# A feed-forward layer in a float32 decoder trunk: fourteen pairs of column blocks computed by halves instead of ten, with another product order and another order of the weight pieces

## The chip, the cores and the metric

The kernel runs on one core of a Trainium2 chip. A core has TensorE (matrix products, PE in the profile; its weight loads are PEld), VectorE (DVE), ScalarE (ACT), GpSimd (POOL) and SyncE (SP, which here only starts transfers). Each engine runs its own instructions in program order and waits on semaphores for the others. The metric is device time in microseconds (us) for one execution; lower is better. PSUM, where matrix products accumulate, is used by banks that hold 128 x 512 float32 each.

## The reference

A decoder trunk of two layers on 512 tokens of 1024 numbers: a recurrent block in layer 0, an RWKV-7 time mixing in layer 1, and behind each a gated feed-forward network with a causal convolution. The change is in the feed-forward network alone:

```python
def _conv_ffn(x, norm, w_up, conv_w, conv_b, w_down):
    h = _rmsnorm(x, norm)
    u = jnp.einsum('btd,df->btf', h, w_up)
    gate = _causal_dwconv(u[..., :D_FF], conv_w, conv_b)
    hid = jax.nn.gelu(gate, approximate=True) * u[..., D_FF:]
    return jnp.einsum('btf,fd->btd', hid, w_down)
```

`D_FF` is 3072, so `w_up` is 1024 x 6144 (3072 gate columns, then 3072 up columns) and `w_down` 3072 x 1024. The convolution runs along the tokens, with three taps.

## The kernel before, in words

**Precision.** Every matrix product is in float32 by three products of rounded operands (`mm3`, L54): a weight w is split into a rounded high part and the rest, `wh` and `wl` (or `hi` and `lo`), and so is x. The split is a cast on ScalarE (L94, or L747 for `hi`) and a subtraction on VectorE (L97, or L748 for `lo`).

**Pairs.** A feed-forward layer is cut into 12 pairs, n = 0 to 11. A pair is 256 gate columns and the 256 up columns that belong to them. A pair is computed in one of two ways.

- `Whole`: four steps G0, U0, G1, U1, where G is gate, U is up and 0 and 1 are the halves of the 1024 rows; 24 matmuls of 128 x 512 in each step.
- `Halves`: the tokens, the 1024 rows and the two kinds of columns (gate and up) are all cut in two, and seven products, numbered 1 to 7, of sums and differences of the halves replace eight (a Strassen-like scheme). Each is 24 matmuls of 128 x 256. `HALVES = (3, 5, 7, 9, 11)` names these pairs, in both layers, so that there are ten.

**Banks in a `Halves` pair.** Products 1, 6, 7 and 4 go one after another into bank A (`accA`), each added to what is there; behind 1, 6 and 7 ScalarE copies the bank to a tile `s[1]`, `s[6]`, `s[7]` (L769). Product 5 and then 3 go into bank F (`accF`), product 2 into bank D (`accD`). VectorE adds D to s[1] (L771), F behind product 5 to s[7] (L775) and F behind product 3 to s[6] (L778); the gate half goes to `gpad` (L776, L782). Then come the convolution (`cv`, L692 and L694), the gelu (`ge`, L695), the product with the up half (L787) and the split of the hidden tile (`hid`, L788 and L789).

**Weights.** `plan` lists all weight pieces in the order in which they are fetched. `weights_load` starts a 512 KB transfer on SyncE's queue (L166) into a `raw` tile and, for two of the five pieces of a `Halves` pair, a second transfer on GpSimd's queue that adds another piece into the tile (L168). The operand of product 6 is the sum of the raw tiles of products 1 and 5 (VectorE, L741), formed in the tile of product 1; GpSimd then adds one more piece into the same tile, for product 3 (L752). So a raw tile serves products 1, 6 and 3 one after another. The tiles of raw, hi, lo, wh and wl all come from one pool of 21 rooms, and a new tile waits until the last reader of its room is done.

**Order.** `products` walks through the list of (pair, product) and prepares the weights of two products ahead. For n = 3, 5, 7, 9, 11 the loop at the end of the layer runs the products of pairs n - 1 (`Whole`) and n up to product 7, and then `down`, the products of hidden columns by `w_down`: its first piece, then products 3 and 4 of pair n (`between`), then its other pieces, at the end of the first half of which the next pair's first products are prepared (`then`). Within this a scheduler settles the order of the instructions on each engine.

## Time and profile before

| | |
|---|---|
| median of 3 runs | 1278.75 us (1278.33 to 1279.27) |
| profiled execution | 1279.1 us |
| its span | 1277.3 us |
| mean granted clock of TensorE | 0.998 |
| transferred | 141.37 MB, 111 GB/s |

The page of the profile gives the busy time of each engine, the span in 40 slices, the DMA queues, the chain of waits that ended last, and the costliest groups of instructions. A row of a timeline is start, length (us), engine, line, operation, what it writes and reads, the tile's shape, how many instructions are merged, and in brackets the time the engine stood idle before it and what it waited for. In a row of a group, the numbers behind the bar are the busy time, the mean length of one in ns, and the idle time of the engine just before. Successive matmuls overlap in the records, so the length of a product is taken as the distance from its first matmul to that of the next product. Names such as `L769` are lines of the kernel before; in the changed kernel the same statements stand a few lines lower (L747 becomes L751, L748 L752, L752 L756, L741 L743, L769 L773, L775 L779, L778 L782).

### The profile page before, as it was taken

To read this page: it belongs to the slowest core of one execution; us is meant where nothing else is said; L and a number is where in the kernel's file an instruction comes from. 1 tells how busy PE (TensorE), PEld (TensorE's weight loads), DVE (VectorE), ACT (ScalarE), POOL (GpSimd) and SP (SyncE) were. 2 spreads that over 40 slices of the span, in tenths; PEclk is the share of its full clock that TensorE was granted. 3 is DMA by queue.
4 is the path that set the end of the run, shared out by engine and by line. 5 is a ranking of instruction groups with operands and counts; after the bars stand their busy time and mean duration, and the time that the engine had idled before them with its cause. 6 is when DMAs were issued, how large, how long until landed. Compare 5 with 4: busy or idle time off the path is not lost. (4 is left out here: it accounts for less than half of the span.)

```text
span 1277.3 us, 22409 instructions
## 1 busy us (share of the span) xinstructions
PE 1256.0 (98%) x9259; PEld 1067.4 (84%) x9259; DVE 929.2 (73%) x1412; ACT 642.8 (50%) x1006; POOL 131.1 (10%) x206
## 2 busy tenths in 40 slices
PE   9999999999999999999999898999999999999998
PEld 8777888989898989877778797778889898989896
DVE  5998678767676767789999967778776666666654
ACT  6797455434343434559845356545644334343442
POOL 3000001010101010010012145310010101000000
PEclk9999999999999999999999999999999999999999
DMA  7312335445454544413222122122345454545431
GB/s 228 109 53 97 98 119 114 158 106 167 97 175 89 181 83 137 141 57 110 67 75 68 35 63 85 50 94 83 127 88 181 83 182 83 182 83 182 98 133 66
DMA packets 117829, 141.37 MB, mean 111 GB/s; under 512 B 10138, under 2 KB 91748, under 8 KB 117600
## 3 DMA queue, kind: packets, MB, share of 16 engines
q1 hardware_dynamic: 100528, 122.44, 29.9%
q0 software_dynamic: 16624, 16.47, 8.3%
q8 instruction: 72, 1.18, 0.4%
q10 hardware_dynamic: 576, 1.05, 0.2%
q14 instruction: 29, 0.24, 0.1%
HBM read 135.41 MB, written 4.52 MB: 110 GB/s over the span
## 5 line engine op out<-in xcount | busy, mean ns | idle before, releaser
L97 DVE TENSOR_TENSOR wl<-raw,wh 128x1024 fp32r<-128x1024 f32 (+1 forms) x161 | 194.4, 1213 | 123.6 <-ACT wh L94 103.8
L94 ACT CAST wh<-raw 128x1024 fp32r<-128x1024 f32 (+1 forms) x161 | 165.9, 1043 | 179.8 <-PE acc L54 40.7
L54 PE MATMUL accU<-xs,wh 128*128 128x512 f32 x448 | 138.6, 391 | 0.0
L54 PE MATMUL accG<-xs,wh 128*128 128x512 f32 x448 | 138.6, 390 | 0.0
L54 PE MATMUL acc<-hid,wh 128*128 128x512 f32 x384 | 117.9, 389 | 0.0
L748 DVE TENSOR_TENSOR lo<-raw,hi 128x1024 fp32r<-128x1024 f32 x70 | 85.5, 1222 | 39.4 <-PE accU L54 32.0
L747 ACT CAST hi<-raw 128x1024 fp32r<-128x1024 f32 x70 | 73.7, 1054 | 60.4 <-PE accU L54 25.3
L54 PEld LDWEIGHTS accU<-xs,wh 128*128 128x128 f32 x448 | 83.7, 188 | 17.1
L54 PEld LDWEIGHTS accG<-xs,wh 128*128 128x128 f32 x448 | 83.7, 188 | 17.0
L54 PE MATMUL accU<-xs,wl 128*128 128x512 f32 x224 | 87.2, 389 | 0.0
L54 PE MATMUL accG<-xs,wl 128*128 128x512 f32 x224 | 87.2, 389 | 0.0
L54 PE MATMUL accA<-xt,hi 128*128 128x256 f32 x480 | 83.5, 277 | 0.0
L54 PEld LDWEIGHTS acc<-hid,wh 128*128 128x128 f32 x384 | 71.4, 188 | 14.3
L54 PE MATMUL acc<-xs,wh 128*128 128x512 f32 x256 | 80.9, 398 | 0.0
L694 DVE SCALAR_TENSOR_TENSOR cv<-gpad,pv,cv 128x512 f32<-128x512 f32 x96 | 69.1, 747 | 13.1 <-ACT cv L692 12.7
L848 PE MATMUL acc<-wh,hid 128*128 128x512 f32 (+1 forms) x200 | 76.2, 381 | 0.0
L849 PE MATMUL acc<-wl,hid 128*128 128x512 f32 (+1 forms) x200 | 76.1, 381 | 0.0
L847 PE MATMUL acc<-wh,hid 128*128 128x512 f32 (+1 forms) x200 | 76.1, 381 | 0.0
L54 PE MATMUL acc<-hid,wl 128*128 128x512 f32 x192 | 74.3, 389 | 0.0
L168 POOL DMA_DIRECT2D raw<-in_ffn_w_up_dram x20 | 25.7, 1285 | 469.8 <-DVE x L863 166.5
L54 PEld LDWEIGHTS accA<-xt,hi 128*128 128x128 f32 x480 | 72.6, 188 | 0.0
L54 PE MATMUL accA<-xt,lo 128*128 128x256 f32 x240 | 66.3, 276 | 0.0
(411 smaller groups left out, 2938.0 us busy)
## 6 DMA issues: line engine op xcount, KB each, us to landing
raw<-in_ffn_w_up_dram SPq DMA_DIRECT2D x106, 512.0 KB, 3.9
raw<-in_ffn_w_down_dram SPq DMA_DIRECT2D x48, 512.0 KB, 4.0
raw<-in_ffn_w_up_dram POOLq DMA_DIRECT2D x30, 512.0 KB, 5.7
raw<-in_rwkv_w_rkv_dram SPq DMA_DIRECT2D x24, 512.0 KB, 3.8
raw<-in_lru_w_in_dram SPq DMA_DIRECT2D x16, 512.0 KB, 4.0
raw<-in_lru_w_out_dram SPq DMA_DIRECT2D x8, 512.0 KB, 3.8
raw<-in_rwkv_w_out_dram SPq DMA_DIRECT2D x8, 512.0 KB, 3.8
xd<-x SPq DMA_DIRECT2D x8, 256.0 KB, 2.1
```

What stands on the lines that cost most here:

```text
L54: mm = lambda *a, **kw: self.nc.tensor.matmul(ps, *a, skip_group_check=more, **kw)
L94: put = (self.nc.vector.tensor_copy if dve else self.nc.scalar.copy)(hi, src)
L97: self.nc.vector.tensor_tensor(lo, src, hi.bitcast(F32), ALU.subtract)
L168: self.nc.gpsimd.dma_start(raw, more, accum_op=ALU.add)
L694: nc.vector.scalar_tensor_tensor(cv, pair.gp[:, e, j : j + T], cw(j), cv, ALU.mult, ALU.add)
L747: nc.scalar.copy(hi, f[p])
L748: tt(lo, f[p], hi.bitcast(F32), ALU.subtract)
L847: nc.tensor.matmul(ps, hh[:, s], wh[:, k, m], start=kk == 0, stop=False)
L848: nc.tensor.matmul(ps, hl[:, s], wh[:, k, m], start=False, stop=False)
L849: nc.tensor.matmul(ps, hh[:, s], wl[:, k, m], start=False, stop=kk == blocks - 1)
```

## The change

`HALVES` becomes `(3, 5, 6, 7, 9, 10, 11)`: pairs 6 and 10 of each layer are computed by halves too. The product order of every `Halves` pair goes from 1, 5, 6, 2, 7 to 1, 2, 5, 6, 7, with 3 and 4 behind as before. In the plan the piece with an addition for product 5 comes first and the piece of product 1 second. The sum for product 6 (L743 after) gets an ordering constraint: it stands behind the last addition of F to s[6] (L782 after) of the pair that precedes. The first matmul of each half product is kept in program order (`pin`). Preparing products for the next pairs (`ahead`) is capped at product 4 of pair n until `soon` is reached in the second half of `down`; `then` only fetches the raw pieces of pair n + 1 when that is a `Halves` pair. In pairs 6 and 10 products 3 and 4 run directly behind product 7, since `down` comes only after odd pairs.

```diff
-HALVES = (3, 5, 7, 9, 11)
+HALVES = (3, 5, 6, 7, 9, 10, 11)
...
-    def mm3(self, ps, w, x, start, stop, more=False):
+    def mm3(self, ps, w, x, start, stop, more=False, pin=False):
...
-        mm(wh, xh, start=start, stop=False)
+        first = mm(wh, xh, start=start, stop=False)
+        if pin:
+            self.tc.keep_in_program_order(first)
...
-                        for first, more in (((0, 0), None), ((1, 1), (1, 0)), ((0, 1), None), ((1, 0), (0, 0)), ((1, 1), None)):
+                        for first, more in (((1, 1), (1, 0)), ((0, 0), None), ((0, 1), None), ((1, 0), (0, 0)), ((1, 1), None)):
...
-                order = ((1, 5, 6, 2, 7), (3, 4))
+                order = ((1, 2, 5, 6, 7), (3, 4))
...
-                        pair.f = dict(zip((1, 5, 2, 7), [self.loaded.pop(i + j) for j in range(4)]))
+                        pair.f = dict(zip((5, 1, 2, 7), [self.loaded.pop(i + j) for j in range(4)]))
...
-                        tt(f[1], f[5], f[1], ALU.add)
+                        add = tt(f[1], f[5], f[1], ALU.add)
+                        for ins in evicted[-1:]:
+                            tc.add_manual_dep(add.ins, ins.ins.name, NOSYNC, reason="behind the pair before")
...
-                        tt(s[6], s[6], bank["F"], ALU.add)
+                        evicted.append(tt(s[6], s[6], bank["F"], ALU.add))
...
-                while made[0] < min(j, len(seq)):
+                while made[0] < min(j, cap[0]):
...
-                    if p == "G0" and n + 1 in HALVES:
+                    if p in ("G0", 5) and n % 2 == 0 and n + 1 in HALVES:
                         self.weights_load(quads[n + 1] + 4)
...
-                    if p == 7:
+                    if p == 7 and n % 2:
                         self.weights_split(behind[n] + 2)
...
+            def fetch(n):
+                if n in HALVES:
+                    self.weights_load(quads[n] + 4)
+
+            def prepare():
+                cap[0] = len(seq)
+                ahead(at[0] + 2)
+
             for n in range(3, 12, 2):
                 products((n, 7))
+                cap[0] = seq.index((n, 4)) + 1
...
-                down(n, 2 * n - 6, 4 if n < 11 else 8, lambda: products((n, 4)), lambda: ahead(at[0] + 2))
+                down(n, 2 * n - 6, 4 if n < 11 else 8, lambda: products((n, 4)), lambda: fetch(n + 1), prepare)
```

TensorE before, in pair 5 of layer 0, at the end of product 2 (bank D) and the start of product 7 (bank A). The number behind a name tells one tile from another; what stands in brackets is the engine whose semaphore is waited for.

```order
L54 MATMUL accD<-xs_1469,hi_2581 128x256 x2
L54 MATMUL accD<-xs_1469,lo_2582 128x256
L54 MATMUL accA<-xt,hi_2612 128x256 [waits Activation_49]
L54 MATMUL accA<-xt,hi_2612 128x256
L54 MATMUL accA<-xt,lo_2613 128x256 [waits DVE_49]
```

Product 7 waits for ScalarE's copy of bank A, with product 2's 24 matmuls between the two products on that bank. TensorE after, in pair 6 of layer 0, at the end of product 6 and the start of product 7, both on bank A:

```order
L54 MATMUL accA<-xt,hi_2960 128x256 x2
L54 MATMUL accA<-xt,lo_2961 128x256
L54 MATMUL accA<-xt,hi_2994 128x256 [waits Activation_49]
L54 MATMUL accA<-xt,hi_2994 128x256
L54 MATMUL accA<-xt,lo_2995 128x256 [waits DVE_49]
```

Product 7 now follows product 6 with nothing between, and its first matmul waits for the copy. TensorE after, in the same pair, from product 7 to product 3 (bank F):

```order
L54 MATMUL accA<-xt,hi_2994 128x256 x2
L54 MATMUL accA<-xt,lo_2995 128x256
L54 MATMUL accF<-xs_1412,hi_3033 128x256 [waits DVE_49]
L54 MATMUL accF<-xs_1412,hi_3033 128x256
L54 MATMUL accF<-xs_1412,lo_3034 128x256
```

Product 3 follows product 7 at once, and waits for VectorE's addition of bank F. ScalarE after, in pair 6 of layer 0: hi_3033 and hi_3063 are the operands of its products 3 and 4, hi_3095 and hi_3125 those of products 1 and 2 of pair 7, and the three copies are those of products 1, 6 and 7.

```order
L773 COPY s<-accA 128x512 [waits PE_49]
L751 CAST hi_3033<-raw_2853 128x1024 [waits DMASW4_49,PE_49]
L751 CAST hi_3063<-raw_2992 128x1024 [waits DMAHW0_49,PE_49]
L751 CAST hi_3095<-raw_3026 128x1024 [waits DMAHW2_49,DVE_49]
L773 COPY s<-accA 128x512 [waits PE_49]
L751 CAST hi_3125<-raw_3028 128x1024 [waits DMAHW3_49]
L773 COPY s<-accA 128x512 [waits PE_49]
```

The copy behind product 6 stands behind three casts. VectorE after, at the same place, with the lo of the same operands and L779, the addition of bank F to s[7]:

```order
L752 TENSOR_TENSOR lo_3034<-raw_2853,hi_3033 128x1024 [waits DMASW4_49,PE_49,Activation_49]
L752 TENSOR_TENSOR lo_3064<-raw_2992,hi_3063 128x1024 [waits DMAHW0_49,DVE_49,Activation_49]
L752 TENSOR_TENSOR lo_3096<-raw_3026,hi_3095 128x1024 [waits DMAHW2_49,PE_49,Activation_49]
L752 TENSOR_TENSOR lo_3126<-raw_3028,hi_3125 128x1024 [waits DMAHW3_49,PE_49,Activation_49]
L779 TENSOR_TENSOR s<-s,accF 128x512 [waits Activation_49]
```

The addition on which product 3 waits stands behind the lo of pair 7's second product. Before, products 7 and 3 had the first piece of `down` between them in every `Halves` pair.

## The prediction

> **What bounds the kernel now.** I read the page first, then the table by windows for a stretch of the first FFN, then the timelines of TensorE, ScalarE and VectorE there. The page's busy times and its slices:

> ```profile
> PE 1256.0 (98%) x9259; PEld 1067.4 (84%) x9259; DVE 929.2 (73%) x1412; ACT 642.8 (50%) x1006; POOL 131.1 (10%) x206
> ...
> PE   9999999999999999999999898999999999999998
> ```

> TensorE is busy for 98% of the span, and the few slices below 9 lie in the middle, in the mixer of layer 1. The windows of the table below are two periods of layer 0's FFN, from the first matmul of pair 4 to that of pair 6, and from there to that of pair 8. A period is a `Whole` pair, a `Halves` pair and 64 matmuls by w_down, and lasts 63.1 us. The columns are busy time with instructions for PE, PEld, DVE, ACT and POOL, then the granted clock, the DMA share and GB/s.

> ```profile
> 264.10:327.20 63.10, 63.10 (x361) 55.59 (x360) 41.69 (x51) 25.05 (x30) 3.79 (x3) 1.00 0.50 134
> 327.20:390.30 63.10, 63.10 (x361) 55.59 (x360) 41.70 (x51) 25.07 (x30) 3.81 (x3) 1.00 0.50 134
> ```

> PE fills both without a hole at full clock. So in the FFN time is what the matmuls take; fewer matmul columns shorten it, and any wait of PE lengthens it, since nothing else has slack to give back. The profiled execution took 1279.1 us for a span of 1277.3; I make the sum against 1279.1 and take off 0.35 at the end, since the median of the runs is 1278.75.

> **What a converted pair gives.** TensorE's timeline gives the length of each product as the distance to the next one's first matmul:

> ```profile
> 264.12 0.62 PE L54 MATMUL accG<-xs,wh 128*128 128x512 f32 x2
> ...
> 285.88 0.40 PE L54 MATMUL accA<-xs,hi 128*128 128x256 f32 x2
> ...
> 288.75 0.40 PE L54 MATMUL accF<-xt,hi 128*128 128x256 f32 x2
> ...
> 291.49 0.39 PE L54 MATMUL accA<-xt,hi 128*128 128x256 f32 x2
> ...
> 294.21 0.39 PE L54 MATMUL accD<-xs,hi 128*128 128x256 f32 x2
> ...
> 297.07 0.40 PE L54 MATMUL accA<-xt,hi 128*128 128x256 f32 x2
> ...
> 299.81 0.63 PE L54 MATMUL acc<-hid,wh 128*128 128x512 f32 x2
> ...
> 305.26 0.40 PE L54 MATMUL accF<-xs,hi 128*128 128x256 f32 x2
> ...
> 308.13 0.40 PE L54 MATMUL accA<-xt,hi 128*128 128x256 f32 x2
> ...
> 310.87 0.63 PE L54 MATMUL acc<-hid,wh 128*128 128x512 f32 x2
> ```

> Pair 4 (`Whole`): 285.88 - 264.12 = 21.76. Pair 5 (`Halves`): products 1, 5, 6, 2, 7 take 2.87, 2.74, 2.72, 2.86, 2.74, products 3 and 4 take 2.87 and 2.74, together 19.54. A converted pair saves 2.22 us of matmul; pairs 6 and 10 in two layers make four, **-8.9 us**. That is the whole gain, and it is there only if PE still never waits.

> **What the new order adds.** Bank A is written by products 1, 6, 7 and 4, and ScalarE copies it out (L769, L773 after) behind each of 1, 6 and 7, so the next of them cannot start before the copy has ended. Before, product 5 lay between 1 and 6, product 2 between 6 and 7, and the first piece of w_down and product 3 between 7 and 4. The copies in pair 5, from ScalarE's timeline, and the two additions of bank F, from VectorE's:

> ```profile
> 294.41 0.59 ACT L769 COPY s<-accA 128x512 f32<-128x512 f32 x1 [2.91 <-PE accA L54]
> ...
> 300.01 0.59 ACT L769 COPY s<-accA 128x512 f32<-128x512 f32 x1 [0.89 <-PE accA L54]
> ```

> ```profile
> 300.63 0.69 DVE L775 TENSOR_TENSOR s<-s,accF 128x512 f32<-128x512 f32 x1 [0.25 <-ACT s L769]
> ...
> 308.33 0.69 DVE L778 TENSOR_TENSOR s<-s,accF 128x512 f32<-128x512 f32 x1 [0.79 <-PE accF L54]
> ```

> A reader of a bank starts 0.20 us after the product's end (294.41 against 294.21, 308.33 against 308.13), and the copy takes 0.59: all 0.79 us lay under product 2. In the order (1, 2, 5, 6, 7) product 7 stands right behind 6. How PE takes up work after a wait for ScalarE shows at one place outside the FFN, ScalarE's row and then TensorE's:

> ```profile
> 122.32 1.99 ACT L94 CAST wh<-raw 128x1024 fp32r<-128x1024 f32 x2
> ```

> ```profile
> 123.42 0.73 PE L54 MATMUL acc<-out,wh 128*128 128x512 f32 x2 [0.37 <-ACT wh L94]
> ```

> The first of the two casts ended about 123.37 (1.05 us each, below), PE went on 0.05 later, and its first two matmuls took 0.73 where they take 0.62 at 264.12. So a wait for a copy that starts at once costs 0.20 + 0.59 + 0.05 + 0.11 = **0.95 us**. [...]

> The places. In pairs 3, 5 and 9 four matmuls of w_down's first piece (96 of pair 4 took 21.76, so four take 0.91 us) stand between 6 and 7 and cover the copy. In pairs 6, 7, 10 and 11 nothing stands between. In pairs 6 and 10 products 3 and 4 also follow 7 directly, with no w_down piece: product 3 writes bank F, which VectorE must first add to s7, and s7 is a copy that starts at product 7's end: 0.20 + 0.59 + 0.03 + 0.69 + 0.05 + 0.11 = 1.67 us at least. So each stretch of two adjacent `Halves` pairs has three waits, at least 0.95 + 1.67 + 0.95 = 3.57 us, against 2.22 saved by that stretch. **Floor: 4 x (3.57 - 2.22) = +5.4 us.**

> It will be more than the floor, because ScalarE and VectorE run in a fixed order and the copies stand behind other work. The prices, from the page and the groups by form of the stretch:

> ```profile
> L748 DVE TENSOR_TENSOR lo<-raw,hi 128x1024 fp32r<-128x1024 f32 x70 | 85.5, 1222 | 39.4 <-PE accU L54 32.0
> L747 ACT CAST hi<-raw 128x1024 fp32r<-128x1024 f32 x70 | 73.7, 1054 | 60.4 <-PE accU L54 25.3
> ...
> raw<-in_ffn_w_up_dram POOLq DMA_DIRECT2D x30, 512.0 KB, 5.7
> ```

> ```profile
> L788 ACT CAST hid<-s 128x512 fp32r<-128x512 f32 x2 | 1.2, 623 | 1.2 <-DVE s L787 1.2
> ...
> L787 DVE TENSOR_TENSOR s<-s,ge 128x512 f32<-128x512 f32 x2 | 1.3, 684 | 0.0
> L695 ACT ACTIVATE ge<-cv 128x512 f32<-128x512 f32 x2 | 1.3, 634 | 1.6 <-DVE cv L694 1.6
> ...
> L782 DVE SCALAR_TENSOR_TENSOR gpad<-accA,rb 128x512 f32<-128x512 f32 x1 | 0.7, 691 | 0.3 <-PE accA L54 0.3
> ```

> *Pair 6, product 6 to 7.* Ahead of the copy on ScalarE stands hi of product 4, whose room comes free at the end of product 5, then hi of pair 7's product 1, which waits for VectorE's lo of product 4. From the end of product 5: 0.20 + 1.05 + 1.22 + 1.05 = 3.5, copy to 4.1, hand-over 0.16: 4.3, where product 6 alone takes 2.72. **1.6 us.**

> *Pair 6, product 7 to 3.* VectorE has lo of pair 7's product 2 ahead of the addition of bank F, and its room comes free one matmul before product 7 ends: 0.1 + 1.22 + 0.69 + 0.16 = **2.1 us**.

> *Pair 7, product 6 to 7.* From the end of pair 6's product 3: s6 + F to 0.9 (0.20 + 0.69); the new hold keeps the sum for product 6 behind it, to 2.1 (1.22, as lo); the s6 product with rb 2.8; at 2.94 product 4 has ended, gpad to 3.6; lo of product 6 to 4.9. Then GpSimd's queue adds product 3's piece into that raw room, landing at 10.6; hi of product 3 to 11.7, ge 12.3, s x ge 13.1, hid 13.7, hi of product 4 14.8, hid 15.4, copy 16.0, hand-over 16.2. Products 4, 1, 2, 5, 6 would have ended at 2.74 + 2.87 + 2.86 + 2.74 + 2.72 = 13.93. **2.2 us.**

> Together 5.9 us per stretch, and pairs 10 and 11 and layer 1 have the same engines' order at these places: 4 x 5.9 = +23.6 us. In pairs 3, 5 and 9 of both layers there is a smaller wait, for the first w_down piece, whose third matmul now stands ahead of product 7. SyncE fetches it when the room of the pair's second product comes free: product 5 before, so that 6, 2 and 7 lay between, and product 2 now, with 5 and 6 between. Pair 5's fetch in layer 0 and in layer 1, and the cast that waits for it:

> ```profile
> 291.57 3.09 SPq L166 DMA_DIRECT2D raw<-in_ffn_w_down_dram  x2
> ```

> ```profile
> 1023.91 3.09 SPq L166 DMA_DIRECT2D raw<-in_ffn_w_down_dram  x2
> ```

> ```profile
> 295.21 1.05 ACT L94 CAST wh<-raw 128x1024 fp32r<-128x1024 f32 x1 [0.22 <-DMA raw<-in_ffn_w_down_dram]
> ```

> ```profile
> 1028.24 1.05 ACT L94 CAST wh<-raw 128x1024 fp32r<-128x1024 f32 x1 [0.90 <-DMA raw<-in_ffn_w_down_dram]
> ```

> The issue stands 0.08 behind product 5's end (291.49), and the piece is there 3.64 or 4.33 later. Counted from product 2's end that gives 0.08 + 3.64 + 1.05 + 1.22 + 0.16 = 6.15, and 6.84 with the later landing, for a matmul that is due at 2.74 + 2.72 + 0.45 = 5.91: 0.2 us in layer 0, 0.9 in layer 1, three times each, **+3.3 us**.

> **The rest of the change** I take at nothing. The other order of the five pieces puts the one with the addition first; its 5.7 us landing has a `Whole` pair or w_down work ahead of it as cover in pairs 3 to 11, and if that cover went, each landing late would stop product 5 by up to 5.7. Four more pairs bring eight plain additions by DMA and four held ones, each some 1.3 us of GpSimd's 131 of 1277. VectorE gains per converted pair three lo and one sum, four times 1.22, less what smaller tiles save: some 47 of a 61 us period against 41.7 of 63.1, so it does not become the bound. The pins keep a product's first matmul in written order and cost no time of their own.

> Sum: 1279.1 - 8.9 + 23.6 + 3.3 = 1297.1, less 0.35: **1296.8 us**, 1.4% slower.

> **Rivals.**

> *Only the floor* (0.16). The casts ahead of the copies come earlier than I walked, since a room or a landing is sooner, and only the bank's own hand-over is left: 1279.1 + 5.4 + 0 to 3.3, less 0.35, so **1284.2 to 1287.5**. For it: the 2.91 us of idle time ahead of the copy at 294.41 show that ScalarE had time to spare. Against it: the spare time was in a pair with w_down work around it.

> *The clock falls* (0.08). Where PE waits often, its granted clock can fall. The windows show both:

> ```profile
> 640.00:644.00 4.00, 3.07 (x12) 2.26 (x13) 3.83 (x9) 2.79 (x3) 0.00 (x0) 1.00 0.19 73
> ```

> ```profile
> 795.00:797.00 2.00, 1.21 (x33) 1.09 (x33) 1.16 (x3) 0.69 (x2) 1.29 (x4) 0.96 0.04 16
> 797.00:799.00 2.00, 2.00 (x44) 1.88 (x47) 1.67 (x3) 0.41 (x2) 0.00 (x0) 0.50 0.03 8
> 799.00:801.00 2.00, 2.00 (x34) 1.79 (x28) 1.07 (x2) 0.26 (x1) 0.00 (x0) 0.69 0.75 132
> ```

> After a single gap near 641 it stayed at 1.00; after a run of gaps near 795 it fell to 0.50 and 0.69 for two windows of 2 us, worth 2 x 0.50 + 2 x 0.31 = 1.6 us. Behind the two longest waits of each stretch, eight times, that makes 13 more: **1309.6 us**. [...]

> *The waits stay under the gain* (0.06): **faster**. If the three waits of a stretch came to less than 2.22 us, that is under 0.74 each, the four saved lengths would win; with none, 1279.1 - 8.9 - 0.35 = **1269.9**. It needs the copy to be done while other matmuls run; for it speaks that the scheduler did find four of w_down in pairs 3, 5 and 9. Against it: with 0.59 for the copy alone and 0.69 for the addition, the floor is 3.57.

> *Landings behind one another* (0.10). GpSimd's additions queue up and land at 7.5, the longest shown here, instead of 5.7:

> ```profile
> DMA to landing us min/median/max: 5.6/5.7/7.5
> ```

> This is the group of the plain additions; pair 7's wait then grows by 1.8, four times that is 7.2: **1304 us**.

> **Numbers.** The forecast, three waits of together some 6 us in each stretch, gets 0.56, and it has a spread of its own, 1289 to 1302; what is left, 0.04, is gain and waits that cancel to within 0.2%, about 2.5 us, which is what a measurement of this kernel can tell from no change. Faster by more: 0.06. Slower: 0.90. The range goes from just under the floor, 1283, to 1304, the late landings; it leaves out the faster cases and the clock's.

> **What would show it.** Right: in the profile after, PE's waits name the copy L773 between products 6 and 7 of pairs 6, 7, 10 and 11, and VectorE's L779 ahead of product 3 of pairs 6 and 10, together some 23 us; a `Halves` pair's products still take 2.7 to 2.9 each. The forecast is wrong if PE is dense there, or if the waits near those places are all 0.9 and 1.7, or if the clock drops, or if PE waits mainly at other pairs.

## The result, and the profile after

The changed kernel takes 1330.6 us in the median (1326.7 to 1333.8) beside 1279.0 of the kernel before on the same chip: 1.0405 times as long, 95% interval 1.0393 to 1.0417. It is slower, as forecast, but by 51.6 us and not by 18. The profiled execution took 1331.64 us.

The page of the profile after:

```profile
span 1329.9 us, 23097 instructions
...
PE 1268.0 (95%) x9547; PEld 1087.7 (82%) x9547; DVE 955.2 (72%) x1440; ACT 658.3 (49%) x1030; POOL 147.1 (11%) x218
...
PE   9999999999899989999899999999999997999788
...
PEclk9999999999999998999999999999999998999889
```

TensorE is down from 98% of the span to 95%, and yet busy for 12.0 us longer than before, although its matmuls should be 8.9 us shorter: it waits, and part of its work runs slower. What it waits for, from the waits of TensorE after (total us, times, longest):

```profile
PE accA L54 <- ACT s L773: 26.2, 8, 6.6
PE accF L54 <- DVE s L779: 7.4, 4, 1.9
```

The two rows are the waits that the forecast named: eight at product 7 behind ScalarE's copy, in pairs 6, 7, 10 and 11, and four at product 3 behind VectorE's addition in pairs 6 and 10, together 33.6 us instead of 23.6. TensorE's timeline after shows that these places are not alike. The bracket holds the wait ahead of the row's matmul; the rows are product 7 of pair 6, product 3 of pair 6 and product 7 of pair 7 in layer 0, product 3 of pair 10 and product 7 of pair 11 there, then product 7 of pairs 6, 7, 10 and 11 in layer 1:

```profile
341.92 0.39 PE L54 MATMUL accA<-xt,hi 128*128 128x256 f32 x1 [1.42 <-ACT s L773]
...
346.78 0.39 PE L54 MATMUL accF<-xs,hi 128*128 128x256 f32 x1 [1.86 <-DVE s L779]
...
365.49 0.38 PE L54 MATMUL accA<-xt,hi 128*128 128x256 f32 x1 [1.64 <-ACT s L773]
...
476.89 0.51 PE L54 MATMUL accF<-xs,hi 128*128 128x256 f32 x2 [1.86 <-DVE s L779]
...
499.90 0.58 PE L54 MATMUL accA<-xt,hi 128*128 128x256 f32 x1 [4.32 <-ACT s L773]
...
1102.57 0.58 PE L54 MATMUL accA<-xt,hi 128*128 128x256 f32 x1 [6.63 <-ACT s L773]
...
1129.51 0.38 PE L54 MATMUL accA<-xt,hi 128*128 128x256 f32 x1 [1.58 <-ACT s L773]
...
1240.21 0.58 PE L54 MATMUL accA<-xt,hi 128*128 128x256 f32 x1 [5.58 <-ACT s L773]
...
1268.55 0.58 PE L54 MATMUL accA<-xt,hi 128*128 128x256 f32 x1 [3.59 <-ACT s L773]
```

The first three are the stretch that the prediction walked through. Four others, at product 7, are two to nearly five times as long as their like there, and the matmul behind each takes 0.58 instead of 0.39 us. The granted clock behind them, from the table by windows (the last number but two of a row; the order is that of the waits of 6.6, 4.3, 5.6 and 3.6 us, then product 3 of pair 10 and of pair 6 in layer 0):

```profile
1102.57:1106.57 4.00, 4.00 (x19) 4.00 (x20) 0.72 (x1) 0.89 (x1) 0.95 (x1) 0.50 0.66 97
499.90:503.90 4.00, 4.00 (x18) 4.00 (x19) 2.56 (x3) 0.90 (x1) 0.00 (x0) 0.50 0.90 174
1240.21:1244.21 4.00, 4.00 (x23) 4.00 (x24) 0.72 (x1) 0.89 (x1) 1.28 (x1) 0.64 0.30 42
1268.55:1272.55 4.00, 4.00 (x18) 4.00 (x19) 2.28 (x3) 0.89 (x1) 0.00 (x0) 0.50 0.02 7
476.89:480.94 4.05, 4.05 (x24) 4.05 (x25) 1.68 (x2) 0.00 (x0) 0.00 (x0) 0.70 0.53 83
346.78:349.75 2.97, 2.97 (x24) 2.97 (x25) 1.68 (x2) 0.00 (x0) 0.00 (x0) 1.00 0.29 46
```

Behind three of the long waits TensorE runs at half its clock for the whole of the next 4 us, and behind the one of 5.6 us for part of them (0.64). So the difference of the two spans, +52.6 us, comes apart like this, by the distances between the first matmuls of the pairs in both traces:

| part | us |
|---|---|
| four pairs by halves, 4 x 2.22 | -8.9 |
| waits at products 7 and 3 in the four stretches of adjacent pairs | +33.6 |
| slower matmuls in these stretches (their lengths grew by 41.18; 41.18 + 8.88 - 33.6) | +16.4 |
| pairs 3, 5 and 9 | +2.3 |
| from layer 0's pair 11 to the mixer of layer 1 (56.95 to 60.73) and from there to layer 1's pair 3 (403.64 to 407.62), all of it in the mixer | +7.8 |
| ahead of the first pair | +1.1 |
| behind layer 1's pair 11 | +0.2 |

The profile counts a wait from the end that it models for the last matmul. By the distance between first matmuls each of the twelve waits is about 0.17 us longer, for example 341.92 - 337.61 - 2.72 = 1.59 beside 1.42 for pair 6 of layer 0; these 2.0 us stand in the row of the slower matmuls. The granted clock of the four stretches, read in windows of 1 us, accounts for 14.0 us of that row.

**Why one stretch has long waits and another not.** The four long waits are those where GpSimd's addition for product 3 lands late. Its issues in pair 6 of layer 0 and of layer 1, from GpSimd's timeline, each with its own time to landing:

```profile
329.93 1.27 POOL L756 DMA_DIRECT2D raw<-in_ffn_w_up_dram  x1 [11.13 <-DVE lo L752]
```

```profile
DMA to landing us min/median/max: 5.6/5.6/5.6
```

```profile
1088.55 1.28 POOL L756 DMA_DIRECT2D raw<-in_ffn_w_up_dram  x1 [13.56 <-DVE lo L752]
```

```profile
DMA to landing us min/median/max: 8.7/8.7/8.7
```

In the other two stretches it lands after 8.4 (pair 11 of layer 0), 9.1 (pair 10 of layer 1) and 7.9 (pair 11 of layer 1); in the ten other places after 5.6 to 5.9. What stands around it in SyncE's queue, layer 0 and then layer 1:

```profile
331.44 3.88 SPq L168 DMA_DIRECT2D raw<-in_ffn_w_up_dram  x4
```

```profile
1085.38 5.37 SPq L168 DMA_DIRECT2D raw<-in_ffn_w_up_dram  x5
```

In layer 0 four loads of pair 7 start from 1.5 us after the addition on. In layer 1 the first of five starts 3.2 us ahead of it, and three more within 1.1 us of it (at 1087.51, 1087.97 and 1088.87). The three other late additions have a load that starts 0.4 us (pair 10 of layer 1) or 0.7 us (pair 11 of both layers) behind them; the ten that land in time have none nearer than 1.5 us. The pair's first matmul was at 329.12 in layer 0 and at 1084.56 in layer 1, so the addition comes 0.8 us after the pair's start there and 4.0 us after it here. VectorE's timeline in layer 1 shows why:

```profile
1083.44 0.74 DVE L856 SCALAR_TENSOR_TENSOR xtok<-acc,rs,xtok 128x512 f32<-128x512 f32 x1
1084.10 1.21 DVE L743 TENSOR_TENSOR raw<-raw,raw 128x1024 f32<-128x1024 f32 x1
1085.23 0.74 DVE L856 SCALAR_TENSOR_TENSOR xtok<-acc,rs,xtok 128x512 f32<-128x512 f32 x1
1086.48 2.36 DVE L752 TENSOR_TENSOR lo<-raw,hi 128x1024 fp32r<-128x1024 f32 x2 [0.51 <-ACT hi L751]
```

The sum for product 6 (L743) stands among the instructions that read w_down's results out of their banks (L856), its lo follows at 1086.48, and only when that lo is formed may GpSimd add into the tile. The new ordering constraint on the sum (called the hold below) does not put it there: in e3_nohold, without it, the sum starts 0.35 us ahead of the pair's first matmul, and here 0.46 us. It is the place that the scheduler gave it. ScalarE, a queue in program order, then waits for the landing with the copy of bank A behind it:

```profile
1097.33 1.99 ACT L751 CAST hi<-raw 128x1024 fp32r<-128x1024 f32 x2 [9.11 <-DMA raw<-in_ffn_w_up_dram]
1100.99 1.04 ACT L751 CAST hi<-raw 128x1024 fp32r<-128x1024 f32 x1 [1.66 <-DVE lo L752]
1101.94 0.58 ACT L773 COPY s<-accA 128x512 f32<-128x512 f32 x1
```

The cast waits 9.11 us, product 6 has ended at 1095.9 (1102.57 less 6.63), and its copy starts 6 us later.

### The profile page after: what moved, and what is told of

Read it like the earlier page. It is cut to its first block, busy times and chain, and to the rows that moved or that the text cites. A ratio compares the mean times of both kernels' runs of the same rounds, so it can differ in the third digit from the quotient of the medians.

```text
span 1329.9 us, 23097 instructions
## 1 busy us (share of the span) xinstructions
PE 1268.0 (95%) x9547; PEld 1087.7 (82%) x9547; DVE 955.2 (72%) x1440; ACT 658.3 (49%) x1030; POOL 147.1 (11%) x218
## 3 DMA queue, kind: packets, MB, share of 16 engines
q10 hardware_dynamic: 576, 1.05, 0.2%
## 4 chain that ended last, share of the span: by engine, by line
PE 36%; DVE 7%; ACT 4%; DMA 3%; issue 2%; POOL 1%; POOLq 0%; DVEq 0%; ACTq 0%
PE acc L54 6%; PE accU L54 4%; PE accG L54 4%; PE accA L54 4%; PE acc L853 3%; PE acc L852 3%; PE acc L851 3%; DMA raw<-in_ffn_w_up_dram 3%; PE accF L54 2%; DVE X L1327 1%; DVE wl L99 1%; PE accD L54 1%; DVE DA L1325 1%; PE s L1441 1%; ACT wh L96 1%
## 5 line engine op out<-in xcount | busy, mean ns | idle before, releaser
L751 ACT CAST hi<-raw 128x1024 fp32r<-128x1024 f32 x98 | 102.2, 1050 | 150.3 <-DVE raw L743 49.6
L752 DVE TENSOR_TENSOR lo<-raw,hi 128x1024 fp32r<-128x1024 f32 x98 | 119.2, 1222 | 73.7 <-ACT hi L751 38.1
L54 PE MATMUL accA<-xt,hi 128*128 128x256 f32 x672 | 126.1, 290 | 26.2 <-ACT s L773 26.2
L54 PEld LDWEIGHTS accA<-xt,hi 128*128 128x128 f32 x672 | 108.9, 200 | 28.3 <-ACT s L773 27.7
L54 PE MATMUL acc<-hid,wh 128*128 128x512 f32 x384 | 117.3, 391 | 1.9 <-ACT wh L96 1.9
L54 PE MATMUL accU<-xs,wh 128*128 128x512 f32 x320 | 99.2, 391 | 0.0
L54 PE MATMUL accG<-xs,wh 128*128 128x512 f32 x320 | 99.2, 391 | 0.0
L54 PE MATMUL accA<-xt,lo 128*128 128x256 f32 x336 | 96.6, 288 | 0.0
L54 PEld LDWEIGHTS acc<-hid,wh 128*128 128x128 f32 x384 | 71.6, 189 | 16.5 <-ACT wh L96 2.3
L54 PE MATMUL acc<-xs,wh 128*128 128x512 f32 x256 | 80.9, 397 | 0.0
L54 PE MATMUL acc<-hid,wl 128*128 128x512 f32 x192 | 73.2, 393 | 0.2
L54 PEld LDWEIGHTS accG<-xs,wh 128*128 128x128 f32 x320 | 59.6, 188 | 12.1
L54 PEld LDWEIGHTS accU<-xs,wh 128*128 128x128 f32 x320 | 59.6, 188 | 12.2
L54 PEld LDWEIGHTS accA<-xt,lo 128*128 128x128 f32 x336 | 67.0, 199 | 0.0
L54 PE MATMUL acc<-mix,wh 128*128 128x512 f32 x192 | 60.6, 399 | 2.2 <-ACT wh L96 2.2
## 6 DMA issues: line engine op xcount, KB each, us to landing
raw<-in_ffn_w_up_dram SPq DMA_DIRECT2D x110, 512.0 KB, 4.1
raw<-in_ffn_w_down_dram SPq DMA_DIRECT2D x48, 512.0 KB, 3.8
raw<-in_ffn_w_up_dram POOLq DMA_DIRECT2D x42, 512.0 KB, 5.8
raw<-in_rwkv_w_rkv_dram SPq DMA_DIRECT2D x24, 512.0 KB, 3.6
raw<-in_lru_w_in_dram SPq DMA_DIRECT2D x16, 512.0 KB, 4.1
raw<-in_lru_w_out_dram SPq DMA_DIRECT2D x8, 512.0 KB, 3.6
raw<-in_rwkv_w_out_dram SPq DMA_DIRECT2D x8, 512.0 KB, 3.4
```

The costliest lines, as they stand in the source:

```text
L54: mm = lambda *a, **kw: self.nc.tensor.matmul(ps, *a, skip_group_check=more, **kw)
L751: nc.scalar.copy(hi, f[p])
L752: tt(lo, f[p], hi.bitcast(F32), ALU.subtract)
```

## The experiments

The theory (A): the time is lost where a bank of products 6 and 7 is handed over without work between, because the copy and the addition stand in order behind casts that wait for a landing; a longer landing lengthens the wait, and the wait lowers the clock. Its first rival (B): the new product order costs it by itself, since nothing stands between products 6 and 7 any more. Lines of code are those of the kernel after.

**e1_ten: the new orders with the old ten pairs.**

```diff
-HALVES = (3, 5, 6, 7, 9, 10, 11)
+HALVES = (3, 5, 7, 9, 11)
```

> The changed kernel with HALVES back to (3, 5, 7, 9, 11): ten pairs by halves, the new product order, piece order and hold alone. [...] Theory B (the order 6, 7 on one bank costs it in any pair): long waits between 6 and 7 here too, 1290 us or more.

1283.2 us, ratio 1.0033 (1.0021 to 1.0045), where A forecast about 1283. No wait of PE in the FFN exceeds 0.2 us. The orders alone cost 4.0 us, most of it in pairs 3 to 9: the four matmuls of w_down between products 6 and 7 take 1.2 to 1.4 us there (0.91 before, and still 0.92 in pair 11). The other 47.6 us need the four converted pairs.

**e2_oldorder: fourteen pairs with the product order of before.**

```diff
-                order = ((1, 2, 5, 6, 7), (3, 4))
+                order = ((1, 5, 6, 2, 7), (3, 4))
```

> The changed kernel with the product order 1, 5, 6, 2, 7 again, fourteen pairs by halves. Theory B (bank A handed from product 6 to 7): the waits between 6 and 7 go, those of 1.86 us between 7 and 3 in pairs 6 and 10 stay, so 1279 - 8.9 + 4 x 1.9 + 2 and up to 9 outside these layers' pairs: 1280 to 1289 us. Theory A (ScalarE's queue and the late landing): in the built order the copy behind product 6 still stands behind the cast for product 3; with a landing 8 to 9 us after its issue, waits of 2 to 5 us before product 7 remain in layer 1's pairs 6 and 10 and in pairs 7 and 11, some at half clock behind them: 1305 to 1320 us.

1326.1 us, 1.037 (1.0353 to 1.0388). B falls: with product 2 between 6 and 7 the kernel is faster than after by only 4.5 us. A's figure was missed as well: waits for the copy fall from 26.2 to 16.5 us, those ahead of product 3 grow from 7.4 to 12.1. Product order is not the lever while the queues behind the banks are as they are.

**e4_noadd3: without the addition for product 3.** The weights of product 3 lack a term here.

```diff
-                        nc.gpsimd.dma_start(f[3], self.plan[i + 2][0], accum_op=ALU.add)
+                        pass
```

> The changed kernel without GpSimd's addition into the raw piece for product 3, so that product 3's weights lack one term; everything else is computed. Theory A (that landing is what the queue on ScalarE waits for): the waits of 3.6 to 6.6 us between products 6 and 7 shrink to 0.8 to 1.6, no half clock: 1288 to 1298 us. Theory B: the bank and the order of ScalarE alone make the waits, so they stay: above 1320 us.

1303.4 us, 1.019 (1.0174 to 1.0205). Its waits of TensorE:

```profile
PE accA L54 <- ACT s L773: 8.4, 8, 1.4
PE accF L54 <- DVE s L779: 7.4, 4, 1.9
```

All four stretches are now alike (1.43, 1.86 and 0.68 us each), so the long waits are the landing's doing: 17.8 us of the 26.2. What stays is the share of the bare hand-over and of the queue order, 15.8 us, and some 8.5 us outside the stretches, behind layer 0's pair 11 and in the mixer. The time lies between the two forecasts, 5 us above A's.

**e6_fill: unused matmuls in the four longest waits.** 32 matmuls of 128 x 256 into bank D between products 6 and 7, 14.5 us of work in all that nothing uses.

```diff
+                    if p == 6 and pair.n in ((6, 10, 11) if last else (11,)):
+                        for k in range(32):
+                            tc.keep_in_program_order(nc.tensor.matmul(pair.bank["D"][:, k % 2], hi[:, 0, 0:P], op[p][0][0], start=False, stop=False, skip_group_check=True))
```

> The changed kernel with 32 extra matmuls of 128 x 256 (about 3.6 us) into bank D between products 6 and 7, in the four places alone where the clock fell: pair 11 of layer 0 and pairs 6, 10 and 11 of layer 1. Bank D has been read by then and its sums are used by nobody. [...]

1322.6 us, 1.0345 (1.0326 to 1.0364): 8 us faster than after with 14.5 us of matmuls more, and the mean clock rose from 0.985 to 0.994. The forecast was 1314 to 1320 us, 2.6 us less than came, if the idle waits make the clock fall, and 1330 or more if they do not. So the slower matmuls are a consequence of the idle waits and not of the pairs. In one place the work did not reach over the wait: 3.0 us were left, and the granted clock there, from 1095.60 to 1102.20 us, was 0.74. The four waits of up to 1.9 us at product 3 were not filled.

**e7_behind: the cast of product 3 behind the copy of product 6**, and one product prepared ahead instead of two.

```diff
-                    nc.scalar.copy(hi, f[p])
+                    cast = nc.scalar.copy(hi, f[p])
+                    if p == 3 and 6 in pair.cp:
+                        tc.add_manual_dep(cast.ins, pair.cp[6].ins.name, NOSYNC, reason="behind the copy")
...
-            def products(upto, more=2):
+            def products(upto, more=1):
```

> The changed kernel with weights prepared one product ahead instead of two, and the cast hi of product 3 ordered behind the copy of bank A after product 6. Nothing is left out. Theory A (the copy waits on ScalarE behind that cast, and the cast for the landing): all eight waits between 6 and 7 fall to the 0.7 us of the run without the addition; the landing is then met by product 3, where the casts ahead of the copy after product 7 may hold it: 1.9 us in layer 0, 2 to 4 in layer 1. Clock full or nearly. 1295 to 1305 us. Rival C (the landing is late enough to stop product 3 by as much as it stopped product 7): the waits move to product 3, 1320 us or more.

1339.5 us, 1.048 (1.0463 to 1.0498). Its waits:

```profile
PE accF L54 <- DVE s L781: 15.0, 4, 3.9
PE acc L54 <- ACT wh L96: 10.7, 7, 2.2
PE accA L54 <- ACT s L775: 9.4, 14, 0.7
PE acc L853 <- ACT wh L96: 8.1, 5, 1.6
```

Every one of the fourteen waits from product 6 to 7 is now 0.67, the idle time of a bare hand-over, in which nothing stands ahead of the copy. But the time went to the next places, 3.6 to 3.9 us ahead of product 3 and a new 1.6 ahead of w_down in every odd pair. The waits moved down the same queue, and the rival's figure was the right one. What preparing one product fewer did by itself was not run.

**e9_later: pair 7's and 11's loads started behind product 7 rather than 5.** Does the landing depend on them?

```diff
-                    if p in ("G0", 5) and n % 2 == 0 and n + 1 in HALVES:
+                    if p in ("G0", 7) and n % 2 == 0 and n + 1 in HALVES:
```

> The changed kernel with the four raw pieces of pair 7 (and 11) fetched two products later, behind product 7 of pair 6 (10) and not behind product 5. Theory A1 (in layer 1 the addition for product 3 lands 8.8 to 9.2 us after its issue because four or five transfers of SyncE start within 3 us of it): with those transfers later it lands within 5.7 to 6.5, and the waits of 6.6 and 5.6 us in layer 1 shrink to 2 to 3.5; 1305 to 1320 us. Rival A2 (it lands late because of its own place in the program, whatever the other queue does): landing 8 to 9 and waits of 5 to 7 us as before, about 1330.

1343.0 us, 1.0503 (1.0482 to 1.0523). The addition of pair 6 in layer 1, with its landing:

```profile
1098.89 1.28 POOL L756 DMA_DIRECT2D raw<-in_ffn_w_up_dram  x1 [14.02 <-DVE lo L752]
```

```profile
DMA to landing us min/median/max: 5.8/5.8/5.8
```

In pairs 6 and 10 of layer 1 it fell from 8.7 to 5.8 and from 9.1 to 6.0: the loads that start around it are the cause there; the nearest one now starts 2.7 us behind the addition of pair 6. In pair 11 it stays at 8.2 and 7.7, with a load of w_down still 0.7 us behind it. No run moved that load alone, but in e3_nohold the addition comes 4.5 and 4.0 us ahead of it and lands after 6.1 and 5.8. The time rose all the same, since the cast of pair 7's first product now waits for the later load with the copy of product 7 behind it:

```profile
1111.11 1.04 ACT L751 CAST hi<-raw 128x1024 fp32r<-128x1024 f32 x1 [3.48 <-DMA raw<-in_ffn_w_up_dram]
1112.57 1.04 ACT L751 CAST hi<-raw 128x1024 fp32r<-128x1024 f32 x1 [0.41 <-DMA raw<-in_ffn_w_up_dram]
1113.52 0.58 ACT L773 COPY s<-accA 128x512 f32<-128x512 f32 x1
```

Product 3 waited 4.7 to 7.5 us for it.

**e3_nohold: without the hold of the sum.**

```diff
-                        for ins in evicted[-1:]:
+                        for ins in ():
```

> The changed kernel without the hold of product 6's sum behind the last addition of F of the pair before. By the built order the sum of pair 7 then stands ahead of pair 7's lo of product 2 and of s7 + F of pair 6, so its own addition by GpSimd for product 3 can start some 3 us earlier, and s7 + F starts 1.2 us later. Theory A: in pairs 7 and 11 the wait between 6 and 7 (1.6, 4.3, 1.6, 3.6 us) falls to 0.7 to 1.5, the wait before product 3 in pairs 6 and 10 rises from 1.9 to about 3, pairs 6 and 10 otherwise as they were: 1320 to 1328 us. If the hold costs nothing: 1330.

1320.0 us, 1.0325 (1.031 to 1.034). The hold costs 10.6 us, and it does so in pairs 7 and 11: product 7 waits 0.67 there in layer 0 and not at all in layer 1. In pairs 6 and 10 of layer 1 waits of 8.3 and 5.4 us stay, with landings of 10.2 and 8.9, so the hold is not the cause there. Product 3 of layer 0 now waits 2.5 and 3.5 us.

**e8_between: pair 7's first product between 7 and 3 of pair 6** (and pair 11's in pair 10), with the old product order, so that no bank is handed over without work between.

```diff
+            for n in (6, 10):
+                seq.remove((n + 1, 1))
+                seq.insert(seq.index((n, 3)), (n + 1, 1))
```

> A version meant to have the gain without the waits: fourteen pairs, the old product order 1, 5, 6, 2, 7, and product 1 of pair 7 (11) between product 7 and product 3 of pair 6 (10). Product 2 lies between 6 and 7, and 2.87 us between 7 and 3. If the waits come only from bank hand-overs and queues that stand on them: the -8.9 us show, less what is lost outside these layers (4 to 9 us in the other fourteen-pair kernels): 1272 to 1282 us. If the late landing of product 3's piece holds the copies all the same, waits of 1 to 4 us stay in four to six places: 1290 to 1310.

1333.1 us, 1.0429 (1.0402 to 1.0456). Neither figure came true. Work between is not enough: product 3 still waits 1.6 to 2.7 us, pairs 7 and 11 at product 7 2.0 to 4.1, w_down 1.6 and then 0.9 to 2.0.

**e10_pair6 and e11_pair10: one stretch only.** `HALVES` is (3, 5, 6, 7, 9, 11) and (3, 5, 7, 9, 10, 11).

> The changed kernel with pair 6 alone added to the old five (pairs 3, 5, 6, 7, 9, 11 by halves). Theory A, block by block from the changed kernel's trace: +3.5 us for pairs 6 and 7 in layer 0, +12.1 in layer 1, 0.4 in each of eight other pairs by halves (3.2), 0.6 ahead of the first pair: 1279 + 19.4, about 1298 us; the 8 us that the changed kernel lost behind layer 0's pair 11 and in layer 1's mixer do not appear, since they come from the late fetches round pairs 10 and 11. Rival: those 8 us come from the new order of fetches in general, then 1302 to 1306.

> The changed kernel with pair 10 alone added to the old five (pairs 3, 5, 7, 9, 10, 11). Theory A: +10.6 for pairs 10 and 11 in layer 0, +14.9 in layer 1, 0.4 in eight other pairs, 0.6 at the start, and the 8 us behind pair 11 of layer 0 and in the mixer: about 1316 us. Rival (those 8 us are general): 1308 to 1312. With the run for pair 6 the two shares should add up to the 51.6 us of the changed kernel within 4.

1299.6 us, 1.0156 (1.0131 to 1.018), and 1316.0 us, 1.0296 (1.0275 to 1.0317). The two excesses, 20.8 and 37.3, less e1_ten's 4.0, which both contain, make 54.1 beside the 51.6 measured: the stretches cost nearly independently. The loss outside the FFN's stretches is absent in e10_pair6 and present in e11_pair10, so it belongs to pair 10.

**e12_between_nohold: e8_between without the hold.**

> The version with product 1 of pair 7 (11) between products 7 and 3 of pair 6 (10) and the old product order, now without the hold of product 6's sum. Theory A: the waits between 6 and 7 in pairs 7 and 11 (2.1, 4.1, 2.0, 4.1 us) fall to under 1, as they did without the hold in the new order, and the half clock behind the longer ones goes: 1312 to 1322 us. If it is another mechanism there, 1328 to 1335. No gain over the kernel before is expected, since the waits of 1.6 to 2.7 us before product 3 and at the first piece of w_down stay.

1303.6 us, 1.0194 (1.0178 to 1.021). Better than expected: only four waits of over 1 us are left in the FFN.

```profile
PE accF L54 <- DVE s L779: 23.1, 4, 7.0
```

VectorE's timeline in pair 6 of layer 0 has the reason for the longest:

```profile
346.59 1.22 DVE L743 TENSOR_TENSOR raw<-raw,raw 128x1024 f32<-128x1024 f32 x1 [5.62 <-DMA raw<-in_ffn_w_up_dram]
...
352.33 0.68 DVE L779 TENSOR_TENSOR s<-s,accF 128x512 f32<-128x512 f32 x1
```

The sum of the next pair, no longer held, stands ahead of the addition of bank F and waits 5.6 us for a landing, with five more instructions behind it before the addition. Held too late it delays product 3's piece; free, it blocks the bank.

**e13_hold7: the hold behind the addition of F to s[7] instead** (`evicted` takes L779 in place of L782), otherwise as e8_between.

> The version with product 1 of pair 7 (11) between products 7 and 3, with product 6's sum held behind s7 + F of the pair before (and not behind s6 + F, nor unheld). Unheld, the sum stood ahead of s7 + F on VectorE and waited for GpSimd's addition to product 5's piece, and product 3 with it: 4.6 to 7.0 us in four places. Theory A: now only hi of product 5 of pair 7, ahead of the copy s7 on ScalarE, still waits for that landing, so product 3's waits fall to about 2 us as with the first hold (1.6 to 2.7), and the half clock goes: 1279 to 1287 us. Rival: the landing of product 5's piece is so late that all of it shows again, 1300 us.

1306.9 us, 1.0229 (1.0203 to 1.0254): missed. Waits at product 3 are 1.4 to 3.3, and w_down waits again. One constraint alone does not clear the queues.

**e14_clear: every step that waits for a landing behind the bank's reader.** On e13_hold7: the sum only behind lo of its own product 5; hi of product 4 of pair 6 and of product 5 of pair 7 behind the copy s[7] of pair 6, and their lo behind the addition of F; the same in pairs 10 and 11.

```diff
+                        tc.add_manual_dep(add.ins, pair.lo5.ins.name, NOSYNC, reason="behind lo of product 5")
...
+                    m = {4: pair.n, 5: pair.n - 1}.get(p)
+                    if m in (6, 10):
+                        tc.add_manual_dep(cast.ins, pairs[m].cp[7].ins.name, NOSYNC, reason="behind the copy")
+                        tc.add_manual_dep(rest.ins, evicted[-1].ins.name, NOSYNC, reason="behind the addition")
```

> The same, with three orders set so that nothing which waits for a landing stands ahead of copy s7 and s7 + F: the casts hi of product 4 of pair 6 and product 5 of pair 7 behind the copy s7 of pair 6, their lo behind s7 + F, and product 6's sum behind lo of product 5 of its own pair. Nothing is left out. Theory A (all of the loss is waits for queued copies and landings and the clock behind them; the four converted pairs do save 8.9 us of matmul time): 1271 to 1279 us, no wait over 1.5 us at products 7 and 3. Rival (fourteen pairs cost as much elsewhere as they save, by fetches and rooms): 1283 us or more with PE waiting for landings at product 5 or at w_down.

1297.7 us, 1.0148 (1.0132 to 1.0163). Theory A's figure was missed by 19 us. But the waits ahead of product 3 are gone, for the first time. Left are those ahead of product 7 (12.5 us, up to 3.4) and 8.6 us outside.

**e15_first: also hi of product 3 of pairs 7 and 11 behind their copy s[6]**, and w_down's first piece split earlier, after product 2.

> The cleared version with two more places cleared in pairs 7 and 11: the cast hi of product 3 behind the copy after product 6, and the first w_down piece split after product 2 and not after product 7. Theory A: the waits of 1.2, 3.1, 2.4 and 3.4 us before product 7 there, the 0.5 at w_down's first piece and the half clock behind the longer ones go, and the feed-forward layers become shorter than before by some 5 us; what then is left is the 8.6 us that the cleared version lost behind layer 0's pair 11 and in the mixer: 1280 to 1285 us. Rival (fetches and rooms bind whatever the order): waits of 1 to 3 us appear at product 3 or 5 instead, 1290 or more.

1290.6 us, 1.0097 (1.0082 to 1.0111), the rival's figure. But the two FFNs are now within 1.3 and 0.4 us of the kernel before; the excess lies outside, 6.0 us behind pair 11 and 3.6 in the mixer.

**e16_pair6: the same orders, pair 10 whole again.**

> The same cleared version with twelve pairs by halves: pair 6 added, pair 10 not. By the run with pair 6 alone nothing is lost behind layer 0's pair 11 then. Theory A: 2 x 2.22 saved, less single waits near 1 us: 1275 to 1278 us, faster than the kernel before. Rival: the saving of pair 6 is eaten by waits at landings, 1279 to 1285.

1278.4 us, 0.9999 (0.999 to 1.0008). The outside loss is gone, and four small waits (1.33, 0.99, 0.52 and 1.62) eat the 4.4 us of two pairs.

**e17_last: the last waits of e16_pair6 taken away.** Hi of pair 7's product 1 behind the copy s[6] of pair 6; w_down's first piece split after product 6, with hi of product 3 and the copy s[7] behind it.

```diff
+                    if p == 1 and pair.n == 7:
+                        tc.add_manual_dep(cast.ins, pairs[6].cp[6].ins.name, NOSYNC, reason="behind the copy")
...
-                    if p == 7 and n % 2:
+                    if p == (6 if n == 7 else 7) and n % 2:
```

> The version with pair 6 alone, and the last waits of its trace taken away by order: hi of pair 7's product 1 behind the copy after pair 6's product 6 (0.5 to 1.3 us at product 7), the first w_down piece split after product 6 of pair 7, hi of product 3 and the copy s7 behind that split (1.0 and 1.6 us at w_down's first piece). Theory A (nothing else is in the way): those 4.5 us go, 1273.5 to 1276 us, faster than the kernel before by 0.2 to 0.4%. Rival: the waits move to product 3 or 5 of pair 7, 1277 to 1280 us.

1276.3 us, 0.9991 (0.9979 to 1.0002): the interval just reaches no change. The profile is that of the fastest of its twelve runs (1273.3 to 1281.7). In it no wait of PE is left in the FFN, and the distance from pair 3 to pair 11 is shorter by 2.2 us in each layer, which is what one pair saves.

**e18_more: the same orders at pairs 4, 6 and 8.** Sixteen pairs by halves, pair 10 whole.

```diff
-HALVES = (3, 5, 6, 7, 9, 10, 11)
+HALVES = (3, 4, 5, 6, 7, 8, 9, 11)
+EVEN = (4, 6, 8)
+ODD = (5, 7, 9)
```

> The version without waits with three even pairs by halves (4, 6 and 8; pair 10 stays whole, since round it the fetches for the next layer are lost), so sixteen pairs by halves in two layers. Theory A: each of six converted pairs gives its 2.22 us as in the run with pair 6 alone, whose trace has no wait there: 1279 - 13.3, some 1264 to 1269 us, 0.8 to 1.1% faster than the kernel before. Rival (with neighbouring stretches converted the fetches and landings of one stretch meet those of the next): waits at landings come back, 1274 to 1285 us.

1264.7 us (1264.3 to 1266.7), 0.9897 (0.988 to 0.9913): faster than both kernels, and by 13.4 us faster than the one before, where six pairs save 6 x 2.22 = 13.3. That the two agree so closely is in part luck: by distance from pair 3 to pair 11 the two FFNs are shorter by 6.30 and 6.18 us, 2.1 us a pair, and layer 1's mixer, which the change does not touch, by 2.5. In that mixer the granted clock of the kernel before was 0.50 from 796.82 to 800.24 us; its mean over the whole span was 0.998, and 0.999 in e18_more. The page of e18_more, and a window from the first pairs of layer 1 on:

```profile
span 1263.1 us, 23423 instructions
...
PE 1242.4 (98%) x9691; PEld 1075.2 (85%) x9691; DVE 962.2 (76%) x1454; ACT 665.5 (53%) x1042; POOL 155.2 (12%) x224
...
PEclk9999999999999999999999999999999999999999
```

```profile
900.00:1250.00 350.00, 349.98 (x2207) 316.26 (x2206) 243.50 (x314) 158.98 (x216) 32.59 (x27) 1.00 0.58 145
```

TensorE is dense at full clock over 350 us, with pairs by halves side by side: the gain is real where no reader of a bank stands behind a step that waits for a transfer. All kernels from e12_between_nohold on also have the old product order, and the next pair's product 1 between products 7 and 3; whether the new order would do as well under the same constraints was not run.

## Why the prediction was right in sign and wrong in size

**The gain, -8.9: right.** By distance from pair 3 to pair 11, e17_last gains 2.2 us for one pair in each layer and e18_more 2.1 for each of three, beside the forecast's 2.22. The gain shows only when nothing waits.

**The hand-over: right.** The copy in pair 6 of layer 0, from ScalarE's timeline after:

```profile
341.28 0.58 ACT L773 COPY s<-accA 128x512 f32<-128x512 f32 x1
```

Product 7, at 341.92, starts 0.06 us after its end. The forecast took it that the copy has to be over by then; the program itself makes product 7 wait for it, and no run shows whether a copy could run beside matmuls on the same bank. The floor was 0.95 per copy. In e7_behind the profile counts 0.67 of idle time, and by distance product 6 takes 234.70 - 231.14 = 3.56 instead of 2.72; with the 0.11 by which the next two matmuls are slower (0.50 for 0.39) that makes the 0.95.

**The stretch that was walked through: right.** Pairs 6 and 7 of layer 0 lose 1.59, 2.12 and 1.80 us by distance (waits of 1.42, 1.86 and 1.64 in the profile) where 1.6, 2.1 and 2.2 were forecast, and the stretch grew by 3.51 us where 5.9 - 2.22 = 3.68 stood.

**The step that failed** is the sentence that carried this price on: "pairs 10 and 11 and layer 1 have the same engines' order at these places: 4 x 5.9 = +23.6 us". They have nearly the same order of instructions and not the same times. The three other stretches wait 7.60, 10.07 and 11.03 us beside 4.92 in the one that was walked through, because the addition for product 3 lands after 7.9 to 9.1 us there and not after the 5.7 of the walk. For pair 6 the walk has no landing at all: in layer 0 the cast for product 3 starts 2.0 us before product 5 ends (335.64 and 337.61), so it holds nothing up, and in layer 1 it starts 4.3 us after that end (1097.33 and 1093.05), with the copy behind it. In pairs 6 and 10 of layer 1 the scheduler's order has the sum among the instructions that read w_down's banks, the addition is issued 3.2 and 1.7 us later in the pair than in layer 0, and so it falls among the loads of pair 7 or 11. In pair 11 of both layers it has a load of w_down 0.7 us behind it. e9_later moved the loads of pairs 7 and 11, and in pairs 6 and 10 the landing was 5.8 and 6.0; e4_noadd3 took the addition away, and all stretches were alike; e3_nohold took the hold away, which shortened the long waits of pair 11 and those of pair 7, and not those of pairs 6 and 10. The waits come to +33.6 (35.6 by distance) in place of +23.6.

**The clock was priced and then left out.** The forecast held late landings (+7.2) and the falling clock (+13) as two rivals of which one or the other comes, with 0.10 and 0.08. They are one chain: landings of 7.9 to 9.1 us came with waits of 3.59 to 6.63, and over the 4 us behind those waits the granted clock was 0.50 to 0.64. Both came, with 10.0 and 16.4 us (12.0 and 14.4 by distance); e6_fill, which fills the waits and brings the mean clock from 0.985 to 0.994, shows the second follows from the first.

**The rest taken at nothing: wrong by 8.9.** 7.8 of it lie between pair 11 of layer 0 and the end of the mixer behind it. e10_pair6 and e11_pair10 show that it belongs to pair 10 being converted. SyncE's waits between 510 and 580 us, before and then after, show a store that stands in its queue ahead of the next weight loads:

```profile
SPq L1719 <- DVE x L863: 33.1, 8, 11.7
```

```profile
SPq L1736 <- DVE x L869: 41.0, 7, 18.8
```

The store waited up to 18.8 us instead of 11.7, and w_down's and the mixer's weights behind it came later. That the queue is the cause is read from the trace alone; no run took it apart. Against it speaks that in e12_between_nohold, which converts pair 10 without this loss, the same store still waits up to 15.3 us; why the loss is absent there stays open.

**Pairs 3, 5 and 9: right**, +2.3 for a forecast of +3.3, at the place that was named (the four matmuls of w_down), but the same in both layers, where 0.2 and 0.9 a pair were forecast.

With the measured terms the forecast's own sum is 1297.1 + 10.0 + 16.4 - 1.0 + 8.9 = 1331.4, beside 1331.64 profiled. The two must agree, since the terms are taken from the same two traces; what shows the causes are the runs.

## What to carry to other kernels

A walk through one instance prices that instance only: before multiplying it, look in every other instance at when the transfer on which the chain rests is issued and what else is started around it. Where matmul products share a bank, put each instruction that waits for a transfer behind the bank's reader on the engine that reads it, all of them at once; one constraint alone, or one more piece of work between, mostly moved the wait to the next place (e7_behind, e8_between, e13_hold7). Price a wait together with the slower matmuls behind it.

## What the runs showed of the hardware that was not expected

The clock can fall behind waits that are each short. Product 3 in e4_noadd3 follows in all four stretches on waits of 1.43 and 1.86 us with product 7 between. Over the 4 us behind it the granted clock was 0.63 and 0.57 in layer 0 and 1.00 twice in layer 1; a row of each:

```profile
346.18:350.20 4.02, 4.02 (x22) 4.02 (x23) 1.68 (x2) 0.00 (x0) 0.00 (x0) 0.63 0.00 1
...
1096.35:1100.30 3.95, 3.95 (x33) 3.95 (x34) 2.45 (x4) 0.00 (x0) 0.00 (x0) 1.00 0.29 46
```

In the kernel after it was 0.70 at 476.89 and 1.00 at 346.78, behind the same wait of 1.86 us. There each of the four waits of 3.59 us and more came with a fall; the falls at product 3 come with single waits of 1.86 us at most, so short waits are not safe either.

```profile
475.07:478.48 3.41, 1.59 (x13) 1.59 (x14) 3.41 (x4) 1.54 (x2) 0.00 (x0) 1.00 0.99 146
...
345.36:348.78 3.42, 2.00 (x16) 2.01 (x17) 3.10 (x4) 1.12 (x2) 0.00 (x0) 1.00 0.75 118
```

TensorE is idle for 1.82 us of the first and 1.42 of the second, because the other 0.44 of that wait lie in the step before; the steps that follow ran at 0.50 and at 1.00. The traces of before and after have 745 such steps at full clock. The 11 with 1.82 us of idle time or more are all followed by a step at 0.50, and of the 734 others, with 1.65 or less, none is. So in these traces short waits add up when they fall into one step: at the fall at 796.82 us in the kernel before, idle times of 1.73 and 0.57 us make 2.30 in the step that ends there.

In the kernel after, the 512 KB addition by GpSimd's queue for product 3 landed after 5.6 to 5.9 us in the ten places where no load of weights on SyncE's queue started within 1.4 us of it, and after 7.9 to 9.1 us in the four where one started within 0.8 us. In e9_later twelve of the fourteen landed after 5.6 to 6.0 us and two after 8.2 and 7.7, in e3_nohold twelve after 5.8 to 6.1 and two after 10.2 and 8.9.
